# Compressed keys ahead of the first sparse branch's keys, block scores of two pairs in one group, value products in the bank of the transposes

## The chip, the cores and the metric

One Trainium2 chip, one of its cores. The time of a kernel is the device time of an execution in microseconds (us); the kernel before took 422.42 us, the median of three executions. Engines are called as in the profile: PE (TensorE, with PEld for its weight loads), DVE (VectorE), ACT (ScalarE), POOL (GpSimd), SP (SyncE, whose queue issues the loads).

## The reference, cut to what matters

A trunk of two layers on 256 positions of width 1024. Layer 0 has three groups of heads: sparse attention (8 query heads, 2 key/value groups, three branches), block attention (8 heads) and attention into a memory of 256 tokens (4 heads). Layer 1 has retention and a memory group. The sparse group, one query block, is where most of the change lies:

```python
kc = nsa_compress(rot(nkc), ...)              # 15 compressed keys and values for 256 positions
s_c = einsum('bqgid,bngd->bgiqn', qb, kc) * scale
p_c = masked_softmax(s_c, cmp_end[None, :] <= t[:, None])
o_c = einsum('bgiqn,bngd->bqgid', p_c, vc)
...                                           # the selected branch: keys ks, values vs -> o_s
...                                           # the window branch:   keys kw, values vw -> o_w
o = gb[:, :, 0] * o_c + gb[:, :, 1] * o_s + gb[:, :, 2] * o_w
```

With 256 positions each position selects all blocks and the window holds all positions, so the second and third branch are causal attention over all 256 keys, with keys and values of their own. Compressed key n is seen from position 16n+31 on. Block attention has one block of 256 positions here and is causal attention too. Each group's output is multiplied by a SiLU gate, and the groups go together through the output projection.

## The kernel before, in words

**Projections.** Weights come in pieces of 128x1024 (512 KB) through SP's queue into tile `raw` (6 slots). ACT rounds a piece to `whi`, DVE subtracts and leaves the rest in `wlo`, and PE makes three products of 512 columns each, high by high, low by high and high by low, into a bank "pj". `big` holds an input's transpose as high and low part; `y` holds a group's gated output, which the output projection (weights `wout`) reads.

**Banks.** There are eight PSUM banks: "pj" three, "s" two, "tr", "t" and "o" one each. `transposes` turns probabilities and puts them into "t"; turned queries and keys go to "tr" (`btr` in the profile; `bt` is "t", `bo` is "o", `bs` is "s"). A bank is one unit for the waits: whoever writes a bank waits for all who read it before.

**Attention.** A pair is two heads. `pair_scores` makes the causal scores of up to two pairs in one group on PE: for each pair 128 queries by 128 keys and 128 queries by 256 keys, for both heads, which run side by side in the two halves of PE. The first pair's scores take both banks "s", the second's "o" and "tr". In `sparse_pairs` the two are the two branches of one pair of heads; in `mem_attention` (memory groups of both layers) two pairs of memory heads; in `block_pairs` one pair each time. `causal_weights` then takes on DVE a masked minimum for each score tile, on ACT the exponential, on DVE the reciprocal of the sum, its product with the branch's gate and the scaling; PE turns the result and ACT copies it to `pt` (the second pair's go to slots 6 and 7 of `v4`). When two pairs have theirs, the value products V(0,1) and V(2,3) follow, for both branches and the compressed values in one bank, and `gated` multiplies the bank by the SiLU gate into `yf`, and rounds it into `y`.

**Compressed branch.** `compress` makes 15 compressed keys and values from one 280-column projection; the keys go into a 128x30 tile `kcbd`, block-diagonal in the two groups, the values into `vcr`. `compressed_scores` makes eight products of all queries with `kcbd` (16 instructions on PE), one softmax over 128x240 on DVE, and turns the result (`pcT`).

**Order.** Nothing runs as it is written. `Plan` records each operation with its engine and what it depends on, and a list scheduler then sets the order on every engine; each engine plays its list in that order, and waits where an operand is not there. The products of the projections are the filler on PE. Every group of other work on PE (scores, transposes, values) has an entry in `HOLDS`, by which the scheduler delays it behind filler that is ready (500 ns for 1). The order of the calls at the end of layer 0 sets rank among groups. All instructions stand on one line of the profile, so places are told by tiles. Names in the order have buffer numbers behind them: `bt_69_129` is "t", `bs_67_127` and `bs_68_128` are the two "s", `v_5_9_69` holds the sparse queries, `s_0_33_93` the sparse keys.

Of the kernel before, what the change touches and what calls it, by code (L numbers as in the profile page):

```python
# [49 lines left out]
class Op:  # L50
# [7 lines left out]
RELAX = 3000  # L58

HOLDS = (  # L60
# [4 lines left out]
)  # L65


# [285 lines left out]
def trunk(  # L353
# [438 lines left out]
    def mem_attention(eqT, kT, v, szT, y):  # L792
        both = pair_scores(WHOLE, *((eqT[:, pr], kT[:, pr]) for pr in range(2)))
        todo, done = [], []
        for pr in range(2):
            p = tl("p", [P, 2, 512], 3)
            pt = tl("pt", [P, 2, 512], 2)
            mx = tl("mx", [P, 2, 2], 3)
            sm = tl("sm", [P, 2, 2], 3)
            ss = both[pr][1]  # L800
            for hh in range(2):
                s = ss[hh]
                V.tensor_reduce(mx[:, hh], s.rearrange("p (a k) -> p a k", a=2), AX.X, ALU.max, negate=True)
                for tok in range(2):
                    a = slice(tok * T, (tok + 1) * T)
                    seen = S.activation(p[:, hh, a], s[:, a], AF.Exp, bias=mx[:, hh, tok : tok + 1],
                                        accum_out=sm[:, hh, tok : tok + 1])
            read.append(seen)
            for hh in range(2):
                V.reciprocal(sm[:, hh], sm[:, hh])  # L810
                for tok in range(2):
                    a = slice(tok * T, (tok + 1) * T)
                    if 2 * hh + tok == 3:
                        S.activation(p[:, hh, a], p[:, hh, a], AF.Copy, scale=sm[:, hh, tok : tok + 1])
                    else:
# [12 lines left out]
    kS = vsw = nq = gates = kcBD = vcR = pcT = eqS = szm = mb = rstdm = rbm = memk = memv = szb = mq = mk = mvt = yb = k1m = v1m = None  # L828

    def sparse_keys():  # L830
        nonlocal kS, vsw
        ps = ps_k
        kS = tl("s2", [P, 2, T], at=0)
        vsw = tl("s2", [P, 2, T], at=1)
        b = bank("tr")
        for tok in range(2):
            r = rotate(ps[tok][:, :256], tabs["k"][0][:, tok], tabs["k"][1][:, tok], 4, 32)
            for i in range(2):
                PE.transpose(b[:, i * T + tok * P : i * T + (tok + 1) * P], r[:, i * P : (i + 1) * P], ident)
            S.activation(vsw[:, tok], ps[tok][:, 256:], AF.Copy, scale=rstd0[:, tok : tok + 1])  # L840
        S.copy(kS, b.rearrange("p (k t) -> p k t", k=2))

    def sparse_queries():
        nonlocal nq
        nq = heads(project(w512, W["nq"], (xh, xl)), "q", 5)

    def compress():
        nonlocal gates, kcBD, vcR
# [16 lines left out]
        V.tensor_scalar(gates, gates, 1.0, None, op0=ALU.add)  # L865
        V.reciprocal(gates, gates)

        kcBD = tl("kcbd", [P, 30])
        G.memset(kcBD, 0.0)
        srep = tl("yf", [P, T], 2)[64:].rearrange("p (g a n) -> p g a n", g=2, a=4)  # L870
        G.memset(srep, 0.0)
        vcR = [tl(f"vcr{i}", [P, 2, 2, 64], 1, F32R) for i in range(2)]
# [28 lines left out]
            PE.matmul(hb[:, 128 + g * 64 : 192 + g * 64], srep[:, g].rearrange("p a b -> p (a b)"),  # L901
                      w2t[64:, 64:128], start=True, stop=True)
        for g in range(2):
            S.copy(kcBD[g * 64 : (g + 1) * 64, g * 15 : (g + 1) * 15], hb[:64, 64 + g * 15 : 79 + g * 15])
        for a in range(4):
            rows = slice(32 * a, 32 * a + 32)
            raw = hb[rows, 128 + 64 * (a % 2) : 192 + 64 * (a % 2)]
            S.copy(vcR[0][rows, a // 2, a % 2], raw)
            V.tensor_tensor(vcR[1][rows, a // 2, a % 2], raw, vcR[0][rows, a // 2, a % 2].bitcast(F32), ALU.subtract)

    def compressed_scores():
        nonlocal nq, gates, kcBD, pcT
        s = bank("s")
        for tok in range(2):
            for pr in range(4):
                c = (tok * 4 + pr) * 30
                PE.matmul(s[:, c : c + 30], nq[:, pr, tok * P : (tok + 1) * P], kcBD, start=True, stop=True)
        sc = tl("sc", [P, 2, 8, 15])
        V.tensor_tensor(sc, s[:, :240].rearrange("p (a h n) -> p a h n", a=2, h=8),
                        cpak[:, C_CMP : C_CMP + 30].rearrange("p (a n) -> p a n", a=2).unsqueeze(2)  # L920
                        .to_broadcast([P, 2, 8, 15]), ALU.add)
        mx = tl("cmx", [P, 2, 8])
        V.tensor_reduce(mx, sc, AX.X, ALU.max)
        V.tensor_tensor(sc, sc, mx.unsqueeze(3).to_broadcast([P, 2, 8, 15]), ALU.subtract)
        pcr = tl("tmp2", [P, 512], 3, F32R).rearrange("p (a h b n) -> p a h b n", a=2, h=8, b=2)
# [5 lines left out]
        V.tensor_tensor(mx, mx, gates[:, :, 0:8], ALU.mult)  # L931
        V.tensor_tensor(mx, mx, cpak[:, C_TMASK : C_TMASK + 2].unsqueeze(2).to_broadcast([P, 2, 8]), ALU.mult)
        V.tensor_tensor(sc, sc, mx.unsqueeze(3).to_broadcast([P, 2, 8, 15]), ALU.mult)
        S.copy(pcr[:, :, :, 0, :15], sc)
        V.tensor_tensor(pcr[:, :, :, 1, :15], sc, pc[:, :, :, 0, :15], ALU.subtract)
        pcT = tl("s2", [P, 2, T], 1, F32R, 4)
        b = transposes([pc[:, tok, 4 * u : 4 * u + 4].rearrange("p h b n -> p (h b n)") for u in range(2) for tok in range(2)])
        S.copy(pcT.rearrange("p u t -> p (u t)"), b)

    def sparse_pairs(*prs):  # L940
        todo, done = [], []
        for i, pr in enumerate(prs):
            both = pair_scores(SPAN, *((nq[:, pr], kS[:, br]) for br in range(2)))
            for br in (1, 2):
                pt, got = causal_weights(both[br - 1][0], gates[:, :, br * 8 + 2 * pr : br * 8 + 2 * pr + 2], i)
# [7 lines left out]
        side_by_side([x for i, br, pt in todo  # L953
                      for x in causal_values(pt, lambda g, kt: vsw[:, kt, (br - 1) * P + g * 64 : (br - 1) * P + g * 64 + 64],
                                             o[:, i * T : (i + 1) * T], False, br == 2, True)], *done)
        for i, pr in enumerate(prs):
            gated(o[:, i * T : (i + 1) * T], szn[:, pr], yn, pr)

# [71 lines left out]
    def block_pairs(*prs):  # L1030

        nonlocal szb, mq, mk, mvt, yb
        if prs[0] == 0:
            yb = tl("y", [P, 2, 4, T], 2, F32R)
        o = bank("o")
        todo, done = [], []
        for i, pr in enumerate(prs):
            pt, got = causal_weights(pair_scores(SPAN, (mq[:, pr], mk[:, pr]))[0][0], None)
            todo += causal_values(pt, lambda hh, kt, pr=pr: mvt[:, kt, (2 * pr + hh) * 64 : (2 * pr + hh) * 64 + 64],
                                  o[:, i * T : (i + 1) * T], i == 0, True, len(prs) > 1)  # L1040
            done.append(got)
        side_by_side(todo, *done)
# [12 lines left out]
    sparse_pairs(2, 3)  # L1055
    memory_scale()
    memory_keys()
    memory_values()
    memory_group()
# [329 lines left out]
```

## Time and profile before

| | |
|---|---|
| three timed executions | 422.81, 422.42, 420.42 us (median 422.42) |
| the profiled execution | 421.01 us, span of its records 419.2 us |
| granted clock | 0.996 mean |
| PE busy | 412.2 us (98%), 2314 products, and as many weight loads |
| DVE, ACT, POOL busy | 315.8 us (75%), 257.8 us (62%), 10.5 us (2%) |
| DMA | 74.20 MB, mean 177 GB/s |

The profile is one execution. Busy time of a product on PE includes some 0.17 us of its flow through the array, so that products that follow each other overlap: what a product costs is the distance from its start to the start of the next. On DVE it is the same with about 0.08 us. A row of the timeline has the start, the busy time, the engine, the operation with its output and inputs, the shape, how many in a row were folded into it, and in brackets idle time ahead of it where there was some.

### The profile page before, as it was taken

How to read it: one execution, taken by the hardware profiler on the slowest of the kernel's cores; microseconds unless marked ns; L12 is line 12 of the kernel's file. 1: busy time of each engine (PE TensorE's matmuls, PEld its weight loads, DVE VectorE, ACT ScalarE, POOL GpSimd, SP SyncE). 2: the span in 40 equal slices, each digit the busy share in tenths (PEclk: the TensorE clock that was granted, in tenths of full speed). 3: DMA queues.
4: the chain of work that ended last, by engine and by line, in shares of the span. 5: the costliest groups of instructions: out<-in, count | busy, mean ns of one | idle time of the engine just before them, and what ended most of it. 6: DMA issues, size and time to landing. Idle time of an engine off the chain costs nothing.

```text
span 419.2 us, 6447 instructions
## 1 busy us (share of the span) xinstructions
PE 412.2 (98%) x2314; PEld 343.9 (82%) x2314; DVE 315.8 (75%) x643; ACT 257.8 (62%) x487; POOL 10.5 (2%) x23
## 2 busy tenths in 40 slices
PE   8999999999999999999999999999999999999994
PEld 8988988888878776778888887888888888888884
DVE  3889999879769758858888995766997487564634
ACT  4876758658859479846464767554745555643612
POOL 0000000000000000000000000100100010010001
PEclk9999999999999999999999999999999999999998
DMA  7989864783500295550776543556455455546202
GB/s 224 400 307 305 264 220 156 222 278 125 175 2 2 59 369 186 168 172 16 233 216 240 166 154 108 180 183 194 147 184 192 156 171 183 168 152 200 102 0 100
DMA packets 36975, 74.20 MB, mean 177 GB/s; under 512 B 3024, under 2 KB 22736, under 8 KB 36944
## 3 DMA queue, kind: packets, MB, share of 16 engines
q1 hardware_dynamic: 36512, 73.27, 53.1%
q10 hardware_dynamic: 432, 0.52, 0.4%
q8 instruction: 18, 0.29, 0.3%
q14 instruction: 13, 0.11, 0.1%
HBM read 72.74 MB, written 1.05 MB: 176 GB/s over the span
## 4 chain that ended last, share of the span: by engine, by line
PE 94%; DMA 3%; DVE 1%; ACT 1%; SPq 0%; issue 0%
PE bpj L349 72%; PE bs L349 9%; PE btr L349 5%; PE bo L349 5%; PE bt L349 4%; DMA raw<-in_wout 2%; DMA raw<-in_w 1%; ACT whi L349 0%; SPq L349 0%; DVE wlo L349 0%; DVE yf L349 0%; ACT p L349 0%; DVE p L349 0%; DVE v L349 0%; DVE rot_b L349 0%
## 5 line engine op out<-in xcount | busy, mean ns | idle before, releaser
L349 DVE TENSOR_TENSOR wlo<-raw,whi 128x1024 fp32r<-128x1024 f32 (+3 forms) x127 | 147.0, 1165 | 54.4 <-ACT whi L349 53.8
L349 ACT CAST whi<-raw 128x1024 fp32r<-128x1024 f32 (+3 forms) x127 | 127.0, 1004 | 72.1 <-PE bpj L349 34.6
L349 PE MATMUL bpj<-whi,big 128*128 128x512 f32 (+1 forms) x496 | 156.2, 388 | 0.0
L349 PEld LDWEIGHTS bpj<-whi,big 128*128 128x128 f32 x496 | 91.2, 188 | 18.1 <-issue 1.4
L349 PE MATMUL bpj<-wlo,big 128*128 128x512 f32 (+1 forms) x248 | 95.8, 386 | 0.0
L349 PE MATMUL bpj<-big,whi 128*128 128x512 f32 (+1 forms) x320 | 79.6, 377 | 0.1
L349 PEld LDWEIGHTS bpj<-big,whi 128*128 128x128 f32 x320 | 53.4, 191 | 8.4 <-issue 0.7
L349 PEld LDWEIGHTS bpj<-wlo,big 128*128 128x128 f32 x248 | 46.6, 188 | 8.7
L349 PEld LDWEIGHTS bpj<-big,wlo 128*128 128x128 f32 x288 | 41.9, 190 | 3.9
L349 PE MATMUL bpj<-big,wlo 128*128 128x256 f32 x288 | 45.0, 284 | 0.0
L349 PE MATMUL bpj<-whi,y 128*128 128x512 f32 x84 | 28.8, 398 | 0.0
L349 ACT ACTIVATE p<-p,mx 128x256 f32<-128x256 f32 (+1 forms) x48 | 21.5, 452 | 2.3 <-DVE mx L349 2.3
L349 PEld LDWEIGHTS bpj<-whi,y 128*128 128x128 f32 x84 | 15.8, 188 | 3.5 <-ACT v L349 0.3
L349 ACT COPY rot_a<-bpj 128x256 f32<-128x256 f32 x32 | 11.8, 369 | 11.1 <-PE bpj L349 9.8
L349 PE MATMUL bpj<-wlo,y 128*128 128x512 f32 x42 | 16.9, 402 | 0.2 <-DVE wlo L349 0.2
L349 PE MATMUL bt<-cst,p 128*128 128x128 f32 x104 | 16.9, 275 | 0.0
L349 PEld LDWEIGHTS bt<-cst,p 128*128 128x128 f32 x104 | 12.7, 140 | 4.8 <-ACT p L349 1.0
L349 DVE TENSOR_SCALAR p<-p,sm 128x256 f32<-128x256 f32 (+1 forms) x48 | 14.3, 323 | 1.0
L349 ACT COPY pt<-bt 128x384 f32<-128x384 f32 (+1 forms) x24 | 12.4, 516 | 3.8 <-PE bt L349 3.6
L349 DVE TENSOR_TENSOR rot_a<-bpj,rot_a 128x256 f32<-128x256 f32 x32 | 13.3, 417 | 1.7 <-ACT rot_a L349 1.5
L349 ACT ACTIVATE v<-bpj,rstd 128x512 f32<-128x512 f32 (+1 forms) x18 | 12.4, 689 | 3.2 <-PE bpj L349 3.1
L349 DVE TENSOR_TENSOR v<-bpj,v 128x512 f32<-128x512 f32 x6 | 4.1, 692 | 8.5 <-PE bpj L349 8.5
(246 smaller groups left out, 510.5 us busy)
## 6 DMA issues: line engine op xcount, KB each, us to landing
raw<-in_w SPq DMA_DIRECT2D x84, 512.0 KB, 4.0
raw<-in_wout SPq DMA_DIRECT2D x28, 512.0 KB, 3.7
raw<-in_w SPq DMA_DIRECT2D x15, 256.0 KB, 6.5
v<-in_xtok SPq DMA_DIRECT2D x4, 512.0 KB, 7.5
raw<-in_w SPq DMA_DIRECT2D x4, 280.0 KB, 5.0
v<-in_w SPq DMA_DIRECT2D x2, 512.0 KB, 4.7
raw<-in_memT SPq DMA_DIRECT2D x2, 512.0 KB, 4.0
raw<-in_memtok SPq DMA_DIRECT2D x2, 512.0 KB, 4.3
```

The source lines that it names most:

```text
L349: getattr(self.engines[op.lane], method)(*args, **kw)
```

## The change

Five things change in layer 0; the fourth (for the memory group) and the numbers of `HOLDS` reach layer 1 too.

1. `compressed_scores` and `kcbd` go. The first sparse branch gets a key tile of its own, 15 columns wider (in the memory of tile `str`), with the compressed keys in its first 15 columns. The first branch's score products grow from 128 to 143 columns and from 256 to 271, and hold the compressed scores beside the others.
2. The softmax of the compressed branch becomes `compressed_weights(u)`, once for the pairs 0 and 1 and once for 2 and 3, each at half the width. The compressed scores leave the banks by eight adds on DVE of 128x2x15 instead of one of 128x240. Each softmax turns two blocks instead of four at once.
3. `block_pairs` makes the scores of its two pairs in one group.
4. The value products of the sparse, block and memory groups go to bank "t" instead of "o".
5. The calls stand in another order, and `HOLDS` has other numbers.

```diff
 HOLDS = (
-    8, 16, 0, 1, 1, 6, 40, 4, 16, 2, 6, 16, 0, 6, 2, 1, 4, 2, 16, 8, 6, 12, 6, 16, 40, 4, 0, 8, 16, 16, 8, 2,
...
+    6, 16, 16, 2, 40, 8, 1, 6, 8, 2, 40, 12, 8, 24, 6, 0, 4, 0, 24, 2, 24, 12, 24, 24, 6, 40, 1, 0, 1, 2, 8, 0,
...
@@ mem_attention
-        o = bank("o")
+        o = bank("t")
@@ sparse_keys
-        kS = tl("s2", [P, 2, T], at=0)
+        kS = [tl("str", [P, 15 + T]), tl("s2", [P, 2, T], at=0)[:, 0]]
...
-        S.copy(kS, b.rearrange("p (k t) -> p k t", k=2))
+        S.copy(kS[0][:, 15:], b[:, :T])
+        S.copy(kS[1], b[:, T:])
@@ compress
-            S.copy(kcBD[g * 64 : (g + 1) * 64, g * 15 : (g + 1) * 15], hb[:64, 64 + g * 15 : 79 + g * 15])
+            S.copy(kS[0][g * 64 : (g + 1) * 64, :15], hb[:64, 64 + g * 15 : 79 + g * 15])
@@
-    def compressed_scores():
...
-                PE.matmul(s[:, c : c + 30], nq[:, pr, tok * P : (tok + 1) * P], kcBD, start=True, stop=True)
...
-        V.tensor_tensor(sc, s[:, :240].rearrange(...), cpak[:, C_CMP : C_CMP + 30]..., ALU.add)
...
+    def compressed_weights(u):
+        hs = slice(4 * u, 4 * u + 4)
+        sc = tl("sc", [P, 2, 8, 15])[:, :, hs]
...
-        b = transposes([pc[:, tok, 4 * u : 4 * u + 4]... for u in range(2) for tok in range(2)])
-        S.copy(pcT.rearrange("p u t -> p (u t)"), b)
+        S.copy(pcT[:, u], transposes([pc[:, tok].rearrange("p h b n -> p (h b n)") for tok in range(2)]))
@@ sparse_pairs
-            both = pair_scores(SPAN, *((nq[:, pr], kS[:, br]) for br in range(2)))
+            s = [[bank(t) for t in g] for g in ("ss", ("o", "tr"))]
+            side_by_side([(s[br][hh][:, c : c + n], nq[pair_half(hh), pr, tok * P : tok * P + P], kS[br][pair_half(hh), :n], True, True)
+                          for br in range(2) for tok, c, n in (((0, 0, 15 + P), (1, 15 + P, 15 + T)), ((0, 0, P), (1, P, T)))[br]
+                          for hh in range(2)])
+            for hh in range(2):
+                V.tensor_tensor(tl("sc", [P, 2, 8, 15])[:, :, 2 * pr + hh],
+                                s[0][hh][:, : 2 * (15 + P)].rearrange("p (a n) -> p a n", a=2)[:, :, :15],
+                                cpak[:, C_CMP : C_CMP + 30].rearrange("p (a n) -> p a n", a=2), ALU.add)
...
-        o = bank("o")
+        compressed_weights(prs[0] // 2)
+        o = bank("t")
@@ block_pairs
-        o = bank("o")
+        both = pair_scores(SPAN, *((mq[:, pr], mk[:, pr]) for pr in prs))
...
-            pt, got = causal_weights(pair_scores(SPAN, (mq[:, pr], mk[:, pr]))[0][0], None)
+            pt, got = causal_weights(both[i][0], None)
...
+        o = bank("t")
@@ the calls
     compress()
+    block_keys()
+    block_gates()
+    sparse_pairs(0, 1)
     memory_queries()
-    compressed_scores()
-    block_gates()
-    block_keys()
+    memory_scale()
+    sparse_pairs(2, 3)
     memory_rows()
-    sparse_pairs(0, 1)
-    sparse_pairs(2, 3)
-    memory_scale()
     memory_keys()
```

What the order makes of it at three places. First PE, where the compressed keys are just made (`hid` by `w`): before, the products with `kcbd` stand a little later.

```order
L349 MATMUL bs_67_127<-hid_83_143,w_0_54_114 64x30
L349 MATMUL bs_67_127<-w_0_54_114,yf_48_108 128x64 x2
...
L349 MATMUL bpj_78_138<-whi_26_86,big_12_72 128x512
L349 MATMUL bpj_78_138<-wlo_30_90,big_12_72 128x512
L349 MATMUL bpj_78_138<-whi_26_86,big_12_72 128x512
L349 MATMUL bs_68_128<-kcbd_82_142,v_5_9_69 128x30 x8
L349 MATMUL bpj_78_138<-whi_26_86,big_12_72 128x512
```

Now, with the keys of branch one in `str_58_118`:

```order
L348 MATMUL bs_67_127<-hid_82_142,w_0_54_114 64x30
L348 MATMUL bs_67_127<-w_0_54_114,yf_48_108 128x64 x2
L348 MATMUL bpj_78_138<-big_12_72,whi_28_88 128x512 x4
L348 MATMUL bpj_66_126<-big_12_72,wlo_32_92 128x256 x4
L348 MATMUL bpj_78_138<-big_12_72,wlo_32_92 128x256 x4
L348 MATMUL bpj_66_126<-big_12_72,whi_25_85 128x512 x2
L348 MATMUL bs_68_128<-str_58_118,v_5_9_69 128x143
L348 MATMUL bs_67_127<-str_58_118,v_5_9_69 128x143
L348 MATMUL bs_68_128<-str_58_118,v_5_9_69 128x271
L348 MATMUL bs_67_127<-str_58_118,v_5_9_69 128x271
L348 MATMUL bo_80_140<-s_0_33_93,v_5_9_69 128x128
```

The eight products of 30 columns are gone, and the first sparse pair's scores stand 14 filler products behind the compressed keys.

Second, PE behind the value products V(0,1). Before:

```order
L349 MATMUL bo_80_140<-v_7_11_71,s_1_34_94 64x256 x2
L349 MATMUL bo_80_140<-v_7_11_71,s_1_34_94 64x128 x2
L349 MATMUL bpj_65_125<-whi_25_85,big_13_73 128x512
L349 MATMUL bpj_65_125<-wlo_29_89,big_13_73 128x512
L349 MATMUL bpj_65_125<-whi_25_85,big_13_73 128x512
L349 MATMUL bpj_66_126<-whi_26_86,big_12_72 128x512
L349 MATMUL bpj_66_126<-wlo_30_90,big_12_72 128x512
L349 MATMUL bs_67_127<-s_0_33_93,v_5_9_69 128x128
```

Now, with the last of four score products of the next pair and the transposes behind them:

```order
L348 MATMUL bt_69_129<-v_7_11_71,s_1_34_94 64x256 x2
L348 MATMUL bt_69_129<-v_7_11_71,s_1_34_94 64x128 x2
L348 MATMUL bs_68_128<-str_58_118,v_5_9_69 128x143
...
L348 MATMUL bo_80_140<-s_0_33_93,v_5_9_69 128x256
L348 MATMUL btr_72_132<-s_0_33_93,v_5_9_69 128x256
L348 MATMUL bt_69_129<-cst_59_119,p_3_63 128x128 x3
L348 MATMUL bpj_78_138<-big_13_73,whi_27_87 128x512
```

And DVE now, where the reads of that bank (`yf` from `bt`) stand behind a `wlo` subtraction:

```order
L348 TENSOR_TENSOR wlo_32_92<-raw_23_83,whi_28_88 128x1024
L348 TENSOR_TENSOR rot_a_44_104<-bpj_66_126,rot_a_44_104 128x256
L348 TENSOR_TENSOR wlo_29_89<-raw_24_84,whi_25_85 128x1024
L348 RECIPROCAL sm_87_147<-sm_87_147 128x2
L348 TENSOR_TENSOR sm_87_147<-sm_87_147,gates_79_139 128x2
L348 TENSOR_TENSOR yf_81_141<-bt_69_129,v_4_8_68 128x256
L348 TENSOR_TENSOR yf_48_108<-bt_69_129,v_4_8_68 128x256
```

Values and transposes now share the bank: the transposes of `p_3_63` come after both `yf`, with the score block between them on PE.

Third, PE at the first products of the output projection (`y_14_74`). Before, with the turned weights of the memory group (`p_1_61`) right ahead:

```order
L349 MATMUL bpj_66_126<-whi_25_85,big_12_72 128x512
L349 MATMUL bt_69_129<-cst_59_119,p_1_61 128x128 x4
L349 MATMUL btr_72_132<-cst_59_119,rot_a_45_105 128x128 x4
L349 MATMUL bpj_78_138<-whi_26_86,y_14_74 128x512
L349 MATMUL bpj_65_125<-whi_26_86,y_14_74 128x512
L349 MATMUL bpj_78_138<-wlo_30_90,y_14_74 128x512
```

Now, from the memory values (`s_6_39_99`) on, with block scores (`v_1_5_65`, `v_2_6_66`) of two pairs in four banks:

```order
L348 MATMUL bt_69_129<-pt_17_77,s_6_39_99 64x256 x4
L348 MATMUL bs_68_128<-v_1_5_65,v_2_6_66 128x128
L348 MATMUL bs_67_127<-v_1_5_65,v_2_6_66 128x128
...
L348 MATMUL bo_80_140<-v_1_5_65,v_2_6_66 128x256
L348 MATMUL btr_72_132<-v_1_5_65,v_2_6_66 128x256
L348 MATMUL bt_69_129<-cst_59_119,p_3_63 128x128 x3
...
L348 MATMUL bpj_66_126<-whi_25_85,big_12_72 128x512
L348 MATMUL bpj_78_138<-whi_26_86,y_14_74 128x512
```

The memory values and both groups of block scores now stand ahead of the first product on `y`, where before they stood behind it.

More of the change, by code (lines that the diff above doesn't have):

```diff
@@ L826, in mem_attention @@
             gated(o[:, i * T : (i + 1) * T], szT[:, i], y, i)
-    kS = vsw = nq = gates = kcBD = vcR = pcT = eqS = szm = mb = rstdm = rbm = memk = memv = szb = mq = mk = mvt = yb = k1m = v1m = None
+    kS = vsw = nq = gates = vcR = pcT = eqS = szm = mb = rstdm = rbm = memk = memv = szb = mq = mk = mvt = yb = k1m = v1m = None
     def sparse_keys():
@@ L847, in compress @@
     def compress():
-        nonlocal gates, kcBD, vcR
+        nonlocal gates, vcR
         ps = project(w280, 0, (xh, xl), 280)
@@ L866, in compress @@
         V.reciprocal(gates, gates)
-        kcBD = tl("kcbd", [P, 30])
-        G.memset(kcBD, 0.0)
         srep = tl("yf", [P, T], 2)[64:].rearrange("p (g a n) -> p g a n", g=2, a=4)
@@ L909, in compress @@
             V.tensor_tensor(vcR[1][rows, a // 2, a % 2], raw, vcR[0][rows, a // 2, a % 2].bitcast(F32), ALU.subtract)
-    def compressed_scores():
[L912 to L916, printed above, removed]
-                PE.matmul(s[:, c : c + 30], nq[:, pr, tok * P : (tok + 1) * P], kcBD, start=True, stop=True)
[L918 to L922, printed above, removed]
+    def compressed_weights(u):
+        nonlocal pcT
+        hs = slice(4 * u, 4 * u + 4)
+        sc = tl("sc", [P, 2, 8, 15])[:, :, hs]
+        mx = tl("cmx", [P, 2, 8])[:, :, hs]
         V.tensor_reduce(mx, sc, AX.X, ALU.max)
-        V.tensor_tensor(sc, sc, mx.unsqueeze(3).to_broadcast([P, 2, 8, 15]), ALU.subtract)
-        pcr = tl("tmp2", [P, 512], 3, F32R).rearrange("p (a h b n) -> p a h b n", a=2, h=8, b=2)
+        V.tensor_tensor(sc, sc, mx.unsqueeze(3).to_broadcast([P, 2, 4, 15]), ALU.subtract)
+        pcr = tl("tmp2", [P, 512], 3, F32R)[:, :T].rearrange("p (a h b n) -> p a h b n", a=2, h=4, b=2)
         pc = pcr.bitcast(F32)
@@ L930, in compressed_scores @@
         V.reciprocal(mx, mx)
-        V.tensor_tensor(mx, mx, gates[:, :, 0:8], ALU.mult)
-        V.tensor_tensor(mx, mx, cpak[:, C_TMASK : C_TMASK + 2].unsqueeze(2).to_broadcast([P, 2, 8]), ALU.mult)
-        V.tensor_tensor(sc, sc, mx.unsqueeze(3).to_broadcast([P, 2, 8, 15]), ALU.mult)
+        V.tensor_tensor(mx, mx, gates[:, :, hs], ALU.mult)
+        V.tensor_tensor(mx, mx, cpak[:, C_TMASK : C_TMASK + 2].unsqueeze(2).to_broadcast([P, 2, 4]), ALU.mult)
+        V.tensor_tensor(sc, sc, mx.unsqueeze(3).to_broadcast([P, 2, 4, 15]), ALU.mult)
         S.copy(pcr[:, :, :, 0, :15], sc)
         V.tensor_tensor(pcr[:, :, :, 1, :15], sc, pc[:, :, :, 0, :15], ALU.subtract)
-        pcT = tl("s2", [P, 2, T], 1, F32R, 4)
-        b = transposes([pc[:, tok, 4 * u : 4 * u + 4].rearrange("p h b n -> p (h b n)") for u in range(2) for tok in range(2)])
-        S.copy(pcT.rearrange("p u t -> p (u t)"), b)
+        if u == 0:
+            pcT = tl("s2", [P, 2, T], 1, F32R, 4)
+        S.copy(pcT[:, u], transposes([pc[:, tok].rearrange("p h b n -> p (h b n)") for tok in range(2)]))
     def sparse_pairs(*prs):
@@ L942, in sparse_pairs @@
         for i, pr in enumerate(prs):
-            both = pair_scores(SPAN, *((nq[:, pr], kS[:, br]) for br in range(2)))
-            for br in (1, 2):
-                pt, got = causal_weights(both[br - 1][0], gates[:, :, br * 8 + 2 * pr : br * 8 + 2 * pr + 2], i)
+            s = [[bank(t) for t in g] for g in ("ss", ("o", "tr"))]
[6 more added lines that the diff above has]
+                                cpak[:, C_CMP : C_CMP + 30].rearrange("p (a n) -> p a n", a=2), ALU.add)
+            for br, spans in enumerate(((slice(15, 15 + P), slice(30 + P, 30 + P + T)), SPAN)):
+                pt, got = causal_weights([[x[:, a] for a in spans] for x in s[br]],
+                                         gates[:, :, (br + 1) * 8 + 2 * pr : (br + 1) * 8 + 2 * pr + 2], i)
                 todo.append((i, br, pt))
                 done.append(got)
-        o = bank("o")
+        compressed_weights(prs[0] // 2)
+        o = bank("t")
         for i, pr in enumerate(prs):
@@ L953, in sparse_pairs @@
         side_by_side([x for i, br, pt in todo
-                      for x in causal_values(pt, lambda g, kt: vsw[:, kt, (br - 1) * P + g * 64 : (br - 1) * P + g * 64 + 64],
-                                             o[:, i * T : (i + 1) * T], False, br == 2, True)], *done)
+                      for x in causal_values(pt, lambda g, kt: vsw[:, kt, br * P + g * 64 : br * P + g * 64 + 64],
+                                             o[:, i * T : (i + 1) * T], False, br == 1, True)], *done)
         for i, pr in enumerate(prs):
@@ L1034, in block_pairs @@
             yb = tl("y", [P, 2, 4, T], 2, F32R)
-        o = bank("o")
+        both = pair_scores(SPAN, *((mq[:, pr], mk[:, pr]) for pr in prs))
         todo, done = [], []
         for i, pr in enumerate(prs):
-            pt, got = causal_weights(pair_scores(SPAN, (mq[:, pr], mk[:, pr]))[0][0], None)
-            todo += causal_values(pt, lambda hh, kt, pr=pr: mvt[:, kt, (2 * pr + hh) * 64 : (2 * pr + hh) * 64 + 64],
-                                  o[:, i * T : (i + 1) * T], i == 0, True, len(prs) > 1)
+            pt, got = causal_weights(both[i][0], None)
+            todo.append((i, pr, pt))
             done.append(got)
-        side_by_side(todo, *done)
+        o = bank("t")
+        side_by_side([x for i, pr, pt in todo
+                      for x in causal_values(pt, lambda hh, kt: mvt[:, kt, (2 * pr + hh) * 64 : (2 * pr + hh) * 64 + 64],
+                                             o[:, i * T : (i + 1) * T], i == 0, True, len(prs) > 1)], *done)
         for i, pr in enumerate(prs):
```

5 rows, old and new, of the table HOLDS are left out of this document.

## The prediction

> **What bounds the kernel now.** I read the page first, from its head, its slices and its chain.
>
> ```profile
> span 419.2 us, 6447 instructions
> PE 412.2 (98%) x2314; PEld 343.9 (82%) x2314; DVE 315.8 (75%) x643; ACT 257.8 (62%) x487; POOL 10.5 (2%) x23
> PE   8999999999999999999999999999999999999994
> PE 94%; DMA 3%; DVE 1%; ACT 1%; SPq 0%; issue 0%
> ```
>
> PE is the bound in every slice between the first and the last: no slice shows a hole, and the chain that ends last is PE's for 94%. So a microsecond taken out of PE's list is a microsecond of the span, as long as DVE, second at 75%, keeps up. Three questions follow: what PE no longer does, which of its few waits go, and where DVE gets tight.
>
> DVE's load differs by place, so I asked for windows of 32 us (columns: window, length, then busy time and count of PE, PEld, DVE, ACT, POOL).
>
> ```profile
> 30.00:62.00 32.00, 32.00 (x189) 28.11 (x188) 31.03 (x60) 20.00 (x31) 0.31 (x1) 1.00 0.79 255
> 94.00:126.00 32.00, 32.00 (x210) 25.42 (x208) 24.44 (x100) 24.34 (x72) 0.00 (x0) 1.00 0.31 101
> ```
>
> From 30 to 62 us DVE is already 97% busy, from 94 to 126, where the sparse pairs stand, 76%. What the first did to PE is in PE's timeline: eight filler products take 2.11 us up to the next start, where 0.23 apiece would be 1.84.
>
> ```profile
> 58.81 2.28 PE L349 MATMUL bpj<-big,whi 128*128 128x512 f32 x8
> 60.92 1.12 PE L349 MATMUL bpj<-big,wlo 128*128 128x256 f32 x8
> ```
>
> That is 0.27 us of stall in a stretch where DVE is full.
>
> **The change part by part.** *a. The products with the compressed keys.*
>
> ```profile
> 73.92 0.40 PE L349 MATMUL bpj<-whi,big 128*128 128x512 f32 x1
> 74.16 1.86 PE L349 MATMUL bs<-kcbd,v 128*128 128x30 f32 x16
> 75.86 0.47 PE L349 MATMUL bpj<-whi,big 128*128 128x512 f32 x1
> 76.18 0.39 PE L349 MATMUL bpj<-wlo,big 128*128 128x512 f32 x1
> ```
>
> Starts of filler products lie 0.23 to 0.24 us apart. From the start of the block at 74.16 to the second product behind it at 76.18 are 2.02 us, of which one filler product is 0.24: the block costs 1.78 us. It goes: **-1.78**.
>
> *b. Wider scores.* A block of eight score products, two heads side by side:
>
> ```profile
> 100.91 0.93 PE L349 MATMUL bs<-s,v 64*128 64x128 f32 x8
> ...
> 101.89 0.38 PE L349 MATMUL bo<-s,v 64*128 64x256 f32 x1
> ...
> 102.11 0.38 PE L349 MATMUL bo<-s,v 64*128 64x256 f32 x1
> ...
> 102.42 0.44 PE L349 MATMUL bt<-cst,p 128*128 128x128 f32 x2
> ```
>
> 256 columns take 0.22 us for a pair that runs side by side (101.89 to 102.11), in one of the two passes of such a product: 0.84 ns a column. Fifteen columns are 0.013 us, four products of the first branch per pair of heads (two sizes, two passes) and four pairs make 16: **+0.20**. No row has a product of this kind over 256 columns. If one of 271 cost two of 256, eight passes would cost 0.22 more each, +1.8; nothing less than zero makes sense for added columns. I take the linear price, nearest to what 128 and 256 columns show.
>
> *c. Block scores of two pairs at once.* Four products alone:
>
> ```profile
> 157.81 0.93 PE L349 MATMUL bs<-v,v 64*128 64x128 f32 x8
> 158.66 0.65 PE L349 MATMUL bt<-cst,p 128*128 128x128 f32 x4
> ```
>
> A block of one pair takes 0.85 us up to the next start; one of two, above, 102.42 less 100.91, 1.51. Two times one pair is 1.70, so each merge saves 0.19, two merges **-0.38**. Zero is the lower bound, if the saving is only the turn into and out of the group and the filler beside it pays it.
>
> *d. The stall at the first products on `y`.*
>
> ```profile
> 154.41 0.95 PE L349 MATMUL bpj<-whi,y 128*128 128x512 f32 x2
> 155.54 0.50 PE L349 MATMUL bpj<-wlo,y 128*128 128x512 f32 x1 [0.18 <-DVE wlo L349]
> 155.88 0.60 PE L349 MATMUL bt<-cst,p 128*128 128x128 f32 x4
> ```
>
> Three products take 1.47 us where 0.71 would do: 0.7 us lost (a little of it is the turn to the transposes). The chain of waits there and SP's queue tell why:
>
> ```profile
> 143.29 0.98 SPq L349 DMA_DIRECT2D v<-in_xtok  x2
> ...
> 145.06 8.10 DMA raw<-in_wout
> 153.18 1.06 ACT whi L349
> 154.26 1.24 DVE wlo L349
> ```
>
> The loads of `xtok` go into `v4` 6 and 7, which hold turned weights for V(2,3), so SP stands until those values are done (before, 143 us), and the first `wout` piece behind it lands 8.1 us later. In the new order the distance from V(2,3) to the first product on `y` grows: 52 products of 512 columns, 27 transposes, 16 scores and 8 memory values stand between, against 31, 12 and 8 scores. At 0.23 and some 0.1 each that is near 20 us against 10; the load, rounding and subtraction need 8.1+1.06+1.24 plus an issue of about 1. The stall goes with 8 us to spare: **-0.7** (0 if the move brings another load late).
>
> *e. DVE.* Its prices, from start to start:
>
> ```profile
> 90.23 2.35 DVE L349 TENSOR_TENSOR wlo<-raw,whi 128x1024 fp32r<-128x1024 f32 x2
> 92.50 0.42 DVE L349 TENSOR_TENSOR rot_a<-bpj,rot_a 128x256 f32<-128x256 f32 x1
> ...
> 106.14 0.35 DVE L349 TENSOR_SCALAR p<-p,sm 128x256 f32<-128x256 f32 x1
> 106.40 0.16 DVE L349 RECIPROCAL sm<-sm 128x2 f32<-128x2 f32 x1
> 106.60 0.16 DVE L349 TENSOR_TENSOR sm<-sm,gates 128x2 f32<-128x2 f32 x1
> ...
> 107.27 0.42 DVE L349 CUSTOM_DVE_ANT_0 p<-btr,cst 128x256 f32<-128x256 f32 x1
> ...
> 107.61 0.28 DVE L349 CUSTOM_DVE_ANT_0 p<-btr,cst 128x128 f32<-128x128 f32 x1
> 107.82 0.08 DVE L349 DVE_READ_ACCUMULATOR2_ANT mx<- 128x1 f32 x1
> ```
>
> A subtraction 1.14, a minimum over 256 columns 0.34, over 128 0.21, a scaling of 256 0.26, a two-column step 0.20. And by shape (busy, mean ns; some 0.08 us of each overlaps the next):
>
> ```profile
> L349 DVE TENSOR_TENSOR sc<-sc,cmx 128x240 f32<-128x240 f32 x2 | 0.8, 410 | 0.1
> L349 DVE SCALAR_TENSOR_TENSOR big<-raw,vec,big 128x256 fp32r<-128x256 f32 x8 | 3.5, 478 | 0.0
> L349 DVE TENSOR_TENSOR hid<-bs,hid 128x30 f32<-128x30 f32 x1 | 0.2, 190 | 0.1
> ```
>
> Eight adds of 30 columns at 0.11 to 0.19 replace one of 240 at 0.33 to 0.41: about +1.0. Each of eight softmax steps is done twice at half width: halving 410 ns at about 1 ns a column takes off some 125, so the second one costs 0.2 less what the first saves, about 0.16 apiece: +1.3. In all +2.3 us on an engine with a quarter free, and nothing on PE as long as it hides.
>
> Where it may not: in the new order the stretch from the subtraction that feeds the filler in front of the second sparse scores to the second `yf` of V(0,1) holds, on DVE, 6 subtractions (6.8 us), 8 gain steps at 0.40 (3.2), 7 sums of `rot_a` and 12 minima of 256 columns at 0.34 (6.5), 12 minima of 128 (2.5), 20 two-column steps (3.9), 14 scalings at 0.21 to 0.26 (3.2), the half softmax (2.0), six of the small adds (0.9), and 2.3 of others: 31.3. PE's rows in the same stretch are 55 products of 512 columns (12.8), 56 of 256 at 0.12 (6.7), 28 transposes at 0.11 (3.1), four score blocks (6.2) and one block of values:
>
> ```profile
> 115.66 1.52 PE L349 MATMUL bo<-pt,s 128*64 128x256 f32 x16
> ...
> 118.41 0.50 PE L349 MATMUL bpj<-whi,big 128*128 128x512 f32 x1
> 118.53 0.76 DVE L349 TENSOR_TENSOR yf<-bo,v 128x256 f32<-128x256 f32 x2 [2.88 <-PE bo L349]
> ```
>
> 2.75 us, so 31.6. DVE would be 99% full there, and it waits for ACT a little too. The nearest row is the 0.27 us lost in the window at 97%. I take **+0.4**; the ends are 0 (a lead in the buffers of `wlo` pays it) and +2 (DVE 98% busy at best, 31.3/0.98 = 31.9, and waits for ACT of 1 to 1.5 us in series).
>
> *f. Bank "t" for values.* The next transposes must wait for both `yf`. The row shows both done at 119.29, 0.9 us after PE left the values at 118.41. Behind V(0,1) a score block (1.5 us) covers that, behind V(2,3) four transposes into another bank and seven products (2.0), behind the memory values a score block (1.5 for the two pairs). Cost 0, if DVE takes `yf` at once; in the stretch of *e* a subtraction (1.14) may stand ahead, which is in its upper end. Uncovered, it would be 0.9 at each of six value groups.
>
> *g. The rest.* Compressed keys must be in the key tile before the first sparse scores: 14 filler products stand between (six of 0.23, eight of 0.12, 2.3 us), against two products, the vcr casts and two small copies on ACT, some 1.4 us by their lengths. Loads are the same bytes in another order. POOL clears twice at half size and has 98% idle.
>
> [...]
>
> **The sum.** -1.78 +0.20 -0.38 -0.7 +0.4 = -2.3 us. The profiled execution took 421.01 us (span 419.2 and 1.8 around it), so its like would take 418.7. That execution was 1.4 below the median of the runs, 422.42; all four average 421.67. I set the forecast on that mean: 419.4.
>
> **The rivals.** *A, the forecast:* the work goes, the stall at `y` goes, DVE costs a few tenths: 418.4 to 420.3. For it: PE without holes, and costs read off starts. Chance 0.48.
>
> *B, DVE becomes the bound around V(0,1):* +1.5 to +3 instead of +0.4, by waits for `wlo` and for bank "t" in one place: 420.5 to 422. For it: 99% by the count, and DVE's list in the new order has a subtraction right ahead of `yf`. Against it: the window at 97% lost only 0.27. Chance 0.30.
>
> *C, slower:* transposes stand behind the reads of bank "t" at all value groups. Six times 0.9 us, and one subtraction of 1.14 ahead: 6.5 us of stall, 419.0+6.5 = 425.5. It decides from 5.5 us on. Against it: at three of the six the order has 1.5 to 2 us of other work between. Chance 0.07.
>
> *D, better:* DVE costs nothing and the small stall at 59 goes too: from the profiled execution, 421.01-2.66-0.27 = 418.1, or less if two merges bring a little more. Chance 0.15. That the change doesn't do what it says (stall at `y` moves to another late load, first sparse scores wait for the compressed keys) gives 421.67-2.0+0.4 to +1.4, that is 420 to 421, and is counted in A and B.
>
> **How the numbers follow.** The likeliest is A: 419.4, with 418.4 to 420.3 its own range. The range to state holds B and D and a scatter of the median, 0.6 us for runs between 420.42 and 422.81: 422.0+0.6 and 417.4-0.6, so 416.8 to 422.6. Outside it are C and little else. A measurement of this kernel can tell about 0.5%, 2.1 us, from no change: faster is below 420.3, slower above 424.5. A and D are faster but for their upper edge (0.57); B and that edge are the same (0.35); slower is C with a little of its neighbours (0.08).
>
> **What would show it.** Right: no `kcbd` products; scores of 271 columns that start 0.23 us apart; no wait ahead of the first products on `y`; PE with under 1 us of stall from the first sparse scores to V(0,1)'s successor. Wrong: a wait on DVE's `wlo` or `yf` in that stretch of over 1.5 us (B), waits of transposes into `bt` for `yf` at several value groups (C), scores of 271 columns that cost twice 256, or a load of memory rows or `wout` that comes late and opens a hole where there was none.

## The result, and the profile after

The changed kernel takes 417.82 us, median of six executions (417.39 to 418.23), the kernel before 421.49, median of six too (420.31 to 422.81): 3.7 us less, ratio 0.9913 with a 95% interval of 0.9889 to 0.9938. The forecast was 419.4 in a range of 416.8 to 422.6. The profiled execution took 417.39 us, span 415.6, against 421.01 and 419.2: 3.6 us less where the working of the sum gave 2.3. The page:

```profile
span 415.6 us, 6431 instructions
PE 408.6 (98%) x2298; PEld 342.9 (82%) x2298; DVE 316.6 (76%) x658; ACT 257.8 (62%) x491; POOL 10.2 (2%) x23
PE   8999999999999999999999999999999999999994
PE 96%; DMA 2%; ACT 0%; DVE 0%; issue 0%
```

PE's busy time fell by the 3.6 us that the span fell by, and its 16 products with `kcbd` are the difference in count. PE is still the bound in every slice but the first and the last, and DVE's share of the chain that ends last falls from 1% to under half of one. DVE is busy 0.8 us longer, with 15 more instructions.

PE's timeline where the compressed keys come into the scores of the first sparse pair:

```profile
71.92 0.97 PE L348 MATMUL bs<-str,v 64*128 64x143 f32 x8
72.72 0.27 PE L348 MATMUL bo<-s,v 64*128 64x128 f32 x1
...
73.48 0.73 PE L348 MATMUL bpj<-big,whi 128*128 128x512 f32 x2
```

The block of 16 products is gone. The first branch's eight now take 0.80 us (71.92 to 72.72), where the narrow ones took 0.76 (100.91 to 101.67 before): 0.04 a block, 0.16 in four. 271 columns take 0.23 us a pass (the two from 72.27 to 72.72), 0.84 ns a column, and 256 took 0.22 (101.89 to 102.11), so columns past 256 cost what the others cost.

PE around V(0,1), where the forecast saw DVE 99% full:

```profile
100.41 1.47 PE L348 MATMUL bt<-v,s 128*64 128x256 f32 x16
101.81 0.97 PE L348 MATMUL bs<-str,v 64*128 64x143 f32 x8
...
103.36 0.55 PE L348 MATMUL bt<-cst,p 128*128 128x128 f32 x3
```

DVE there, and windows of 16 us with the columns as before:

```profile
100.31 1.22 DVE L348 TENSOR_TENSOR wlo<-raw,whi 128x1024 fp32r<-128x1024 f32 x1
...
101.93 0.76 DVE L348 TENSOR_TENSOR yf<-bt,v 128x256 f32<-128x256 f32 x2
```

```profile
78.00:94.00 16.00, 16.00 (x115) 13.67 (x115) 15.46 (x64) 15.66 (x44) 0.00 (x0) 1.00 0.42 133
94.00:110.00 16.00, 16.00 (x122) 13.40 (x121) 15.62 (x51) 13.70 (x38) 0.00 (x0) 1.00 0.73 223
```

DVE is 97% and 98% busy, and PE waits for it nowhere: both `yf` are done at 102.69, and the transposes into the same bank come at 103.36, behind the score block. At the first product on `y`:

```profile
159.16 0.40 PE L348 MATMUL bpj<-whi,y 128*128 128x512 f32 x1
159.39 0.49 PE L348 MATMUL bt<-cst,p 128*128 128x128 f32 x3
159.64 0.47 PE L348 MATMUL bpj<-wlo,y 128*128 128x512 f32 x1
```

No wait: the stall of 0.7 us is gone.

What the working did not hold is in PE's turns. A stretch is a run of scores, values, transposes or compressed products between fillers. For each, one can take the time from the last filler's start ahead of it to the second filler's start behind it, less what the products in it take at their steady distance (0.227 us for 512 columns, 0.119 for 256, 0.109 for a transpose, and for a pair of score products 0.107 and 0.214, an estimate at about 0.84 ns a column; the rows have 0.11 and 0.22, and by their starts a block leaves 0.02 to 0.05 us less, in both kernels alike). A product of 512 columns is busy for 0.40 us, 0.17 longer than that distance; that these 0.17 us are flow through the array is my reading of the rows, and no run shows it. What is left over, summed over all such stretches of the layers 0 and 1, is 7.4 us before and 6.0 after. Of the 1.4 us between them some 0.3 stand in transposes beside the stall at `y`, and so belong to that stall, and 0.1 in the block with `kcbd`, which is part of term a; 0.9 to 1.0 is in scores and values. Transposes alone leave next to none elsewhere (0.01), a block of scores 0.38 to 0.43, a block of values 0.33 to 0.41, scores straight behind values 0.56 for the two. Besides the stretch with `kcbd`, the kernel before has 16 stretches with scores, values or small products behind the warm-up, the changed one 14. One of the two that went is at V(0,1), where the next scores now follow with no filler between. The other is at the block scores. In the kernel before, two of their four groups already stood right beside the memory values:

```profile
162.01 0.93 PE L349 MATMUL bs<-v,v 64*128 64x128 f32 x8
162.86 1.95 PE L349 MATMUL bo<-pt,s 128*64 128x256 f32 x16
164.74 0.93 PE L349 MATMUL bs<-v,v 64*128 64x128 f32 x8
```

So the four groups and the memory values made three stretches, which leave over 1.52 us; now they make two, with 0.96.

My theory was then: **a turn of PE from whole-array products into half-array ones (scores with 64 rows, values with 64 columns) and back costs 0.4 us whatever is done inside, and what the change brought beyond the forecast is fewer turns.** The rival: turns cost little, and the new order saves waits.

### The profile page after: what moved, and what is told of

It reads as the page before. It is cut to its first block, busy times and chain, and to the rows that moved or that the text cites. A ratio compares the mean times of both kernels' runs of the same rounds, so it can differ in the third digit from the quotient of the medians.

```text
span 415.6 us, 6431 instructions
## 1 busy us (share of the span) xinstructions
PE 408.6 (98%) x2298; PEld 342.9 (82%) x2298; DVE 316.6 (76%) x658; ACT 257.8 (62%) x491; POOL 10.2 (2%) x23
## 4 chain that ended last, share of the span: by engine, by line
PE 96%; DMA 2%; ACT 0%; DVE 0%; issue 0%
PE bpj L348 74%; PE bs L348 7%; PE bt L348 7%; PE btr L348 5%; PE bo L348 2%; DMA v<-in_xT 2%; DMA raw<-in_w 1%; ACT p L348 0%; ACT big L348 0%; ACT whi L348 0%; DVE p L348 0%; DVE v L348 0%; DVE rot_b L348 0%; DVE ss L348 0%
```

## The experiments

Where an order is said to be frozen, the scheduler's result is taken as it is, and the edit then moves, parts or adds rows of one engine's list.

**The changed kernel again**, as a base.

> The changed kernel once more, unedited, beside the next three on the same chip. All theories: 417.4 to 418.2 us, as before, and PE's list without a stall of over 0.1 us behind the first 15 us.

417.86 us (417.48 to 418.63). The median is as expected; one run of four lies above, and the trace has a wait that the expectation ruled out:

```profile
150.06 0.66 PE L348 MATMUL bt<-cst,p 128*128 128x128 f32 x4 [0.21 <-ACT pt L348]
```

Transposes into bank "t" stand for ACT's copy of those before them, which costs 0.27 us in that stretch. The first profile of the changed kernel has no such wait, so it comes and goes. It matters below, where this trace is the base.

**Score blocks parted.**

```diff
+for op in [o for o in pe if o.kind == 2 and len(o.calls) == 8]:   # the 8 score blocks of two pairs
+    two = self.part(op, 4)                                       # second pair on its own
+    ahead = [o for o in pe[pe.index(op) + 1 :] if not o.kind][:2]  # the next two fillers
+    ...                                                          # go between the two
```

> The changed kernel with its order frozen, but each of the 8 score blocks of two pairs is parted: first pair, two filler products, second pair. Same products, same operands, 8 more turns of PE from filler into half-array products and back. Theory 1 (a turn there and back costs 0.38 to 0.42 us whatever is done inside, and the gain beyond the forecast came from fewer turns): +8 x 0.4 = +3.2 us, about 421.0. The forecast's own price of a merge, 0.19: +1.5 us, about 419.3. Theory 2 (the order saves waits, turns cost nothing): within 0.3 us of the changed kernel.

420.49 us (420.27 to 420.71), 2.6 above the base, span 2.8 above: 0.33 to 0.35 us a turn. That is under the theory's 0.4, well over the forecast's 0.19, and far from nothing. PE has no other wait in this trace that the base lacks, but the base has the 0.27 us that this trace lacks. PE's rows show the price without it, here at the first of the eight blocks:

```profile
71.80 0.97 PE L386 MATMUL bs<-str,v 64*128 64x143 f32 x8
72.70 0.73 PE L386 MATMUL bpj<-big,whi 128*128 128x512 f32 x2
...
74.22 0.74 PE L386 MATMUL bpj<-big,wlo 128*128 128x256 f32 x4
```

From the block's start to the filler behind it are 2.42 us, against 1.56 (71.92 to 73.48) in the changed kernel; two fillers are 0.45 of that, so the turn costs 0.41. All eight blocks give 0.39 to 0.41, 3.2 us in all, which is the theory's size. The rival theory had the time within 0.3 us of the changed kernel.

**Only the two block score blocks parted**, the merge of the forecast's term c undone.

> The changed kernel, order frozen, with only the two block score blocks parted: first pair, two filler products, second pair. This undoes the forecast's term c alone, on the same banks. Theory 1 with the price of the run that parted eight blocks (0.35 us each): +0.7 us, about 418.5. The forecast's price (0.19 each): +0.4 us, about 418.2. The difference is to be read in the trace, from the last filler ahead of each block to the second behind it.

419.10 us (417.87 to 419.66), on another chip than the base; with that scatter the time alone does not size it. PE's rows do:

```profile
147.35 0.60 PE L386 MATMUL bt<-cst,p 128*128 128x128 f32 x4
147.88 0.93 PE L386 MATMUL bs<-v,v 64*128 64x128 f32 x8
148.74 0.73 PE L386 MATMUL bpj<-whi,big 128*128 128x512 f32 x2
149.40 0.37 PE L386 MATMUL bo<-v,v 64*128 64x128 f32 x1
...
151.77 1.95 PE L386 MATMUL bt<-pt,s 128*64 128x256 f32 x16
```

and the same place in the changed kernel:

```profile
147.71 0.60 PE L348 MATMUL bt<-cst,p 128*128 128x128 f32 x4
148.24 0.93 PE L348 MATMUL bs<-v,v 64*128 64x128 f32 x8
149.00 0.27 PE L348 MATMUL bo<-v,v 64*128 64x128 f32 x1
...
151.72 0.65 PE L348 MATMUL bt<-pt,s 128*64 128x256 f32 x4
```

From the transposes to the memory values are the same products: 4.42 us with the block parted, 4.01 without, 0.41 for one turn. One sees both halves of it: the first pair's scores take 0.86 up to the filler and 0.76 up to more scores, and the two fillers take 0.66 where 0.46 would do. So PE loses 0.1 on leaving the half-array products, 0.1 between the first filler and the second, 0.1 on the step back into them, and 0.1 more on the first products behind that step. The second block gives 0.41 too. In these traces the price comes with the step between whole-array and half-array products, not with every change of products: transposes between fillers (whole array) leave 0.01, and the 16 whole-array products with `kcbd`, which lie 0.112 us apart, take 1.80 and so nothing beside that, where half-array blocks leave 0.4. Scores straight behind values, a change from one half-array form to the other, leave 0.56 for the two, some 0.25 less than two blocks apart. What in PE takes the 0.4 us no run shows; they show the price only.

**The products of 30 columns put back.**

```diff
+[nq[:, q, tok] x kS[0][:, :30] for tok in range(2) for q in range(4)] -> bank s, one filler ahead of the transposes before pair 1's scores
```

> The changed kernel with its order frozen, and eight products of all queries with 30 columns of the key tile put back between two filler products ahead of the second sparse pair's scores; their results are overwritten and used by nobody. The forecast's term a: +1.8 us, of it 1.7 in 16 steps and 0.1 for the turn, about 419.6. If such products hid behind weight loads or waits nearby, less than +1.

419.48 us, 1.6 above the base (span 1.6). In PE's rows:

```profile
77.33 1.86 PE L385 MATMUL bs<-str,v 128*128 128x30 f32 x16
79.04 0.48 PE L385 MATMUL bpj<-big,whi 128*128 128x512 f32 x1
79.36 0.49 PE L385 MATMUL bt<-cst,p 128*128 128x128 f32 x3
```

2.03 us with one filler in it, 1.80 for the block, as in the kernel before. Term a stands.

**More work for DVE** in the full stretch.

```diff
+2 x V.tensor_reduce(busy, nq as 128x1024, max)   # dead, ahead of the compressed softmax of pairs 0 and 1
```

> The changed kernel with its order frozen, and two dead reductions over 1024 columns on DVE (about 1.1 us each, 2.2 us in all) ahead of the compressed softmax of the first two pairs, in the stretch where DVE has no idle time. Theory 1 (DVE is full there but PE has a lead, and the narrowest is the 0.5 us between the second yf of V(0,1) with the scaling behind it and the transposes that need them): PE stalls by 1.2 to 1.9 us, 419.0 to 419.7. Theory 2 (the lead in the buffers is over 2 us, DVE is no limit there): less than +0.4 us.

419.79 us, 1.9 above the base. DVE's added step, then ACT's rows and PE's waits:

```profile
87.75 2.45 DVE L385 TENSOR_REDUCE busy<-v 128x1 f32<-128x1024 f32 x2
```

```profile
91.08 0.30 ACT L385 ACTIVATE sc<-sc 128x120 f32<-128x120 f32 x1 [1.99 <-DVE sc L385]
...
91.69 0.46 ACT L385 COPY v<-bt 128x384 f32<-128x384 f32 x1
```

```profile
90.39 1.09 PE L385 MATMUL bpj<-big,whi 128*128 128x512 f32 x4
92.20 0.55 PE L385 MATMUL bt<-cst,p 128*128 128x128 f32 x3 [0.71 <-ACT v L385]
...
93.99 0.52 PE L385 MATMUL bpj<-big,wlo 128*128 128x256 f32 x3
95.20 0.55 PE L385 MATMUL bt<-cst,p 128*128 128x128 f32 x3 [0.70 <-ACT v L385]
```

Of 2.37 us added (87.75 to DVE's next start at 90.12) PE loses 0.9 and 0.85 (92.20 less 90.39 less 0.93; 95.20 less 93.99 less 0.36). So the lead of PE's list over DVE there is about 0.6 us. It is not spent at `yf`, as I expected, but by way of ACT: its exponential of the compressed softmax stands 1.99 us for DVE's subtraction, the copy out of bank "t" is queued behind it, and PE's next transposes wait for that bank. The second wait is the next such copy. The size came out as expected, the place did not. (The profiled execution, 420.01 us, has one more wait, of 0.87 us near 27 us, for POOL's `rstd`; neither profile of the unedited changed kernel has it, and it lies ahead of the edit.) DVE was at the edge, and the order stays on the right side of it.

**Values in bank o again**, the second change of bank alone. Run twice.

```diff
-o = bank("t")
+o = bank("o")      # the order of every engine as with "t"
```

> The changed kernel with its order on every engine frozen, but all value groups accumulate in bank o, as before the change, and the second pair's scores use o too. Theory 1 (the bank by itself is worth little; what it does is let scores stand right behind values): a score block that stands right behind values now waits in its second half for both yf, about 0.15 us at V(0,1) and at the memory values, and the memory values wait for the minima of the first block pairs' scores in o, 0.5 to 1 us: +0.8 to +1.5 us in all, about 419. If the bank is the main gain of the change: +2 us or more. If it is nothing: within 0.3 us of the changed kernel.

417.98 us; its profiled execution took 420.16, with waits of 1.2 us near 26 us that have nothing to do with the bank.

> The changed kernel with values in bank o once more, order frozen, beside the kernel with two score blocks parted, on the same chip. Its first trace had waits of 1.1 us more than the changed kernel (0.75 ahead of and behind the memory values, 0.23 behind V(0,1)), its times did not show them. If the waits are real in each execution: 1.1 us above the changed kernel, 0.4 above the parted one, about 418.9. If they come with a late start only: level with the changed kernel, 417.9, and 0.6 below the parted one.

418.55 us (418.23 to 419.27). The second trace, PE behind V(0,1) and the next scores:

```profile
100.58 1.47 PE L399 MATMUL bo<-v,s 128*64 128x256 f32 x16
101.97 0.97 PE L399 MATMUL bs<-str,v 64*128 64x143 f32 x8
102.90 0.37 PE L399 MATMUL bo<-s,v 64*128 64x128 f32 x1
...
103.76 0.55 PE L399 MATMUL bt<-cst,p 128*128 128x128 f32 x3
```

From values to transposes 3.18 us instead of 2.95: the second half of the scores waits for `yf`, 0.23. At the memory values it is 0.29 behind and 0.15 ahead of them, 0.67 in all; in the first trace 1.1. The times do not show it clearly. The first run's other times (417.95 to 418.01) are level with the base, on another chip. The second run stood beside the parted blocks' 419.10 on one chip and is 0.55 below them, which is what was expected if there were no such waits; by the traces, 0.82 for the parted blocks against 0.67, it should be 0.15 below. So the bank by itself is worth 0.7 to 1.1 us in the traces and 0.1 to 0.7 in the medians, and I cannot say it closer. What bank "t" does is let scores stand straight behind values without a wait.

**HOLDS all zero**, another order of the same work.

> The changed kernel with all numbers of HOLDS zero: same work, another order. Counted off the order, PE has 16 excursions into scores, values and compressed products behind the warm-up, against 14 of the changed kernel and 17 of the one before. Theory 1 (turns) with the prices of each kind read off the traces: +0.6 us, 418.4, and whatever waits show in the trace come on top. Theory 2 (the numbers' gain is in waits alone): PE's time outside visible waits is that of the changed kernel.

419.45 us, 1.6 above the base, which ran on another chip. The stretches of scores, values and small products leave over 6.1 us against the base's 5.7. The base's 5.7 holds its wait of 0.27; without it the difference is +0.7, near the +0.6 expected. The rest is waits, so here both theories have a part:

```profile
49.25 0.40 PE L344 MATMUL bpj<-wlo,big 128*128 128x512 f32 x1
49.99 0.33 PE L344 MATMUL bo<-cst,rot_a 128*128 128x128 f32 x1 [0.35 <-DVE rot_a L344]
```

0.5 us goes here for a rotation that DVE has not finished, and 0.16 a little ahead of it. Transposes near 26 us that wait for POOL's `rstd` leave 0.4 over; as those products wait 0.87 us in one run of the changed order and not at all in the base, this need not be due to the new order. Some 0.3 us I can't place.

**One part of the change in the kernel before: values in bank t**, scheduled anew.

> The kernel before with one part of the change: values accumulate in bank t; the scheduler sets the order anew, with the same HOLDS. The order has 17 excursions as before, none of scores behind values joined but one. Theory 1: no gain from turns, so within 0.7 us of the kernel before, but for new waits of transposes for yf, 0 to 2 us. If bank t is what pays: 1.5 us or more faster than before.

421.20 us against 422.00, ratio 0.9988 (0.9974 to 1.0002): no gain that can be told from nothing. The stretches with scores and values leave over what they do in the kernel before, within 0.05 us. Alone, the bank is not what pays.

**The stall at `y` alone, in the kernel before.**

```diff
 SP: raw<-in_wout x4
+SP: v<-in_xtok x2
+SP: v<-in_grow
-SP: (the three loads ahead of the first wout)
```

> The kernel before, its order on every engine frozen, but SyncE issues the two loads of xtok and the one of grow behind the first four pieces of wout instead of ahead of them. The forecast's term d alone: the stall of 0.7 us ahead of the first products on y goes, 0.4 to 1.0 us faster than the kernel before, and its times scatter less if the late landing is what scatters them. If the stall had another cause (the subtraction itself, or loads that crowd): no change.

422.15 us against 422.00, ratio 0.9996 (0.9981 to 1.0011). In the trace the stall is gone:

```profile
156.36 0.70 PE L388 MATMUL bpj<-whi,y 128*128 128x512 f32 x2
156.90 0.39 PE L388 MATMUL bpj<-wlo,y 128*128 128x512 f32 x1
157.13 0.60 PE L388 MATMUL bt<-cst,p 128*128 128x128 f32 x4
```

0.77 us instead of 1.47. But this execution (422.26) has a wait that the first profile of before has not:

```profile
43.48 0.29 PE L388 MATMUL bpj<-whi,big 128*128 128x280 f32 x1
44.29 0.40 PE L388 MATMUL bpj<-whi,big 128*128 128x280 f32 x1 [0.52 <-DVE rot_a L388]
```

0.68 us for a bank that DVE's rotation still reads. The list up to there is that of the kernel before, word for word. The kernel with values in "t" has the same wait (0.69 us, 421.67). So I profiled the kernel before twice more.

> The kernel before once more, unedited, for a second profiled execution. If its times scatter by waits that come and go near the start, executions near 422 us show a wait of 0.5 to 0.8 us of PE near 43 us (products of 280 columns that wait for the rotation on DVE) that the first profile, 421.01 us, does not have; the stall ahead of the first products on y (0.7 us) should be there either way.

> The same again, a third profiled execution, with the same expectation: the wait near 43 us in executions near 422 us, and the stall ahead of the first products on y in all.

They took 421.50 and 420.52 us, and neither has the wait near 43. PE at the first products on `y`, in the one and in the other:

```profile
154.73 1.08 PE L349 MATMUL bpj<-whi,y 128*128 128x512 f32 x2
155.99 0.50 PE L349 MATMUL bpj<-wlo,y 128*128 128x512 f32 x1 [0.18 <-DVE wlo L349]
156.33 0.60 PE L349 MATMUL bt<-cst,p 128*128 128x128 f32 x4
```

```profile
154.55 0.71 PE L349 MATMUL bpj<-whi,y 128*128 128x512 f32 x2
155.10 0.40 PE L349 MATMUL bpj<-wlo,y 128*128 128x512 f32 x1
155.34 0.60 PE L349 MATMUL bt<-cst,p 128*128 128x128 f32 x4
```

0.9 us of stall in the second execution, none in the third; I had expected it in all. It comes with the landing of `wout`: ACT's cast of the first piece, which waits for it, starts at 153.18 in the first execution, 153.63 in the second and 152.63 in the third. The three traces give a mean stall of 0.5. That is too little for the time of the run above to show, which allows a gain of up to 0.8. As the stall can be absent with the order unedited, one trace without it does not show that moving the loads removed it. That the kernel before takes 422 us where the wait near 43 is there is likely from the two traces that have it, and not shown for the kernel before itself. None of the traces of the changed kernel and of those with its order has it, though two of them (more work for DVE, values in bank o) wait 0.9 and 1.0 us near 27 and 28 us for POOL. It fits that the changed kernel scatters over 1.2 us in all its runs and the kernel before over 3.

## Why the prediction was right, point by point

The direction, the mechanism (PE's work sets the time) and the range held. The range says little, though: it reached from 416.8 to 422.6, so the kernel before, unchanged, lay inside it. The likeliest case, A (418.4 to 420.3), did not happen; what happened is the better case, D, which had a chance of 0.15: DVE cost nothing, the stall near 59 us went, and the time came out a little below its 418.1. The sum, 2.3 us, was 1.3 too small against the traces. Against the first profile of before:

| term | forecast | measured | from |
|---|---|---|---|
| a, products with `kcbd` | -1.78 | -1.8 | put back: block 1.80, time +1.6 |
| b, wider scores | +0.20 | +0.16 | 0.80 against 0.76 us a block |
| c, block scores merged | -0.38 | -0.56 | 1.52 less 0.96 left over, memory values included; parted in the new order: 0.41 each |
| d, stall at `y` | -0.7 | -0.7 | 0.5 in the mean of three executions of before; in the time, not to be told from nothing |
| e, DVE | +0.4 | 0 | no wait; lead of about 0.6 us |
| f, bank t | 0 | 0 | no wait for `yf` in the changed kernel |
| turns at the sparse groups and memory scores | none | -0.4 | 2.85 less 2.44 left over |
| stall near 59 us | in D alone | -0.27 | not there after |
| the first 15 us | none | +0.4 | the same work on PE is reached 0.4 us later; 0.0 to 0.8 in the other traces of the changed order |

That makes -3.2 of -3.6; 0.4 us stays unplaced.

- **Term c was mis-sized.** I priced a merge as the difference of blocks up to the next start, 2 x 0.85 less 1.51. That holds the 0.2 us that fall inside the blocks and leaves out 0.1 on the filler ahead and 0.1 on the filler behind. The measured price is twice that, 0.41. Two merges did not bring 0.82 all the same, since two of the four groups already stood beside the memory values in the kernel before.
- **The joins that the order makes were not priced.** The fences of the order show scores straight behind V(0,1), but I read that as cover for `yf` only. It also saves a part of a turn: 0.56 for the two in place of some 0.8. At the memory values scores and values were joined before the change too, so nothing is gained there beyond term c.
- **Term e erred to the careful side.** The count of 31.3 us of DVE in 31.6 was right (97 to 98% busy), and a row at 97% that had lost 0.27 was a fair neighbour, but how full an engine is does not say what it costs. What counts is PE's lead, and that had 0.6 us. Two steps at half width do cost DVE more than one at the whole: a subtraction of 120 columns takes 0.19 us from start to start (87.61 to 87.80), and one of 240 took 0.33 before (77.16 to 77.49), 0.05 less than two of them. This cost PE nothing, for the same reason. The split added less than the 2.3 us of the working: DVE's busy time rose by 0.8.
- **Rival B** did not happen; the added 2.4 us on DVE show that it was 0.6 us away. **Rival C** did not either: the transposes at V(0,1) stood 0.67 us behind the end of both `yf`.
- **The base.** I set the forecast on the mean of four executions, 421.67; the median over all later runs of the kernel before is near 422, so the gain in time is a little larger than in the traces.

## What to carry to other kernels

Where PE is the bound, count its turns between whole-array and half-array products, and price a turn there and back from the last filler ahead to the second behind, since part of it falls on the fillers (0.2 of the 0.4 us here). Here a merge of two small groups saved a whole turn, 0.4 us, and scores straight behind values some 0.25, more than half of one; for that the two must not share a bank that is still being read, which cost 0.23 us at V(0,1) with values in bank "o". A neighbour engine at 98% cost nothing here, because its consumer had a lead of 0.6 us: measure the lead by adding dead work, not by the share. Look at more than one trace before you count a stall as gained or lost.

## What the runs showed of the hardware

A half-array block between fillers costs 0.33 to 0.43 us beside its products, with no more for 32 records in it than for 8, scores straight behind values 0.55 to 0.61 for the two, and transposes in the whole array 0.01. Scores of 271 columns cost per column what 256 do, 0.23 us against 0.22. Stalls came and went between executions on an unchanged order: the kernel before has 0.7, 0.9 and 0 us at the same products on `y`, the changed one 0 and 0.2 at the transposes near 150 us.
